# Output products of a feed-forward half: new planner ranks for the left blocks' parts and for squares and stores of a finished tile

## The chip, the cores and the metric

The kernel runs on one core of one Trainium2 chip. TensorE (PE) multiplies, VectorE (DVE) and ScalarE (ACT) work on tiles in SBUF and PSUM, GpSimd (POOL) and SyncE (SP) mostly issue DMAs. Each engine works through its own list of instructions in order. The metric is the time of one execution on the device, in microseconds; smaller is better. Three runs of the kernel before gave 2675.55, 2676.26 and 2680.1 us, a median of 2676.26 us.

## The reference

One layer of a diffusion backbone on 1024 latent tokens and 256 context tokens, width 1024. A feed-forward half, a mixer of a gated short convolution and attention, and a second feed-forward half, each behind an RMS norm with a shift, scale and gate. Cut to what matters here:

```python
def rms_norm(x, g):
    y = xf * lax.rsqrt(jnp.mean(xf * xf, axis=-1, keepdims=True) + EPS)
    return (y * g.astype(jnp.float32)).astype(x.dtype)

def swiglu(h, w_in, w_out):
    a, b = jnp.split(h @ w_in, 2, axis=-1)
    return (jax.nn.silu(a) * b) @ w_out          # D_FF = 2816 -> 1024

x = x + 0.5 * ml[2] * swiglu(modulate(rms_norm(x, norm1_g), ml[0], ml[1]), ffn1_w_in, ffn1_w_out)
... # mixer: reads rms_norm(x, norm2_g)
x = x + 0.5 * ml[8] * swiglu(modulate(rms_norm(x, norm3_g), ml[6], ml[7]), ffn2_w_in, ffn2_w_out)
return rms_norm(x, final_g)
```

The change touches the products with `w_out` of the two feed-forward halves and, in the first, what follows when a tile of the new `x` is done: its store to DRAM and its square, which the mixer's norm sums up.

## The kernel before, in words

**Numbers.** All products are in float32 with float32r operands. An operand is split into two parts: a rounded high part, made by a cast on ACT, and the rest, made by a subtraction on DVE (`split`, line 197). A product is then three matmuls: high by high, high by low, low by high. So every operand block costs one cast on ACT and one subtraction on DVE before PE can use it.

**The output product.** `row_products` computes `hidden @ w_out` (hidden dimension 2816 = 22 blocks of 128, 1024 tokens, 1024 outputs) in Winograd's form with seven half-size products instead of eight, in the order 2, 1, 4, 6, 5, 7, 3. Each product runs over 11 block rows `j`; a block row has a left block (of the weights, or of a sum of weight quarters) and a right block (of the hidden values, or of a sum of their quarters), both 128x512. PE does 12 matmuls per block row: four output tiles, three matmuls each. `operands` yields, for each pair of block rows, the parts of the left block (tiles `wl` and `wh`, alternating) and of the right block (tiles `rh` for the cast and `rl` for the subtraction; in product 3 other tiles). The left blocks of products 2, 1, 4 and 7 are loaded by SP into `raw` (7 forms a difference of two loads on DVE). Those of 5, 6 and 3 come from `ws`: a load by SP and accumulating DMAs by POOL, and for 6 and 3 a negated copy on ACT between them (`ws<-ws`). `sums` forms the sums of hidden quarters in place (`hid<-hid,hid`) and issues the `ws` steps. When a product ends, `add` on DVE (`x<-ps,gate_l,x`) adds its four PSUM tiles, scaled by the gate, to the tiles of `x` that it belongs to.

**After a product, first half only.** `after1` is called after each pair of block rows and at the end of each product. When the last product for a group of four tiles of `x` has been added, `done` stores each tile to DRAM on SP (`xd<-x`) and calls `mix.square`: a square on ACT into a tile named `sq_acc` (the first of a token block) or `sq`, and for all but the first and the last an addition to `sq_acc` on DVE. C0 and C1 are the two blocks of 512 tokens; `done` is called after product 1 for tiles 0 to 3 of C0, after product 7 for tiles 4 to 7 of C0 and of C1, and after product 3 for tiles 0 to 3 of C1. The norm of C0 (`norms2`) begins after product 7, that of C1 (`norm1`) inside the mixer's first products, after product 3. The second half calls `row_products` with `after3`, which has no squares of this kind; its last product is done in two halves.

**What sets the order.** The instructions are not issued in the order of the text. A planner replays the program on a model of the engines and places them greedily: when an engine comes free, of the instructions that are ready the one with the lowest rank goes next. The rank is a running number in the order of the text. Inside `tc.high_priority(n)` the numbers begin n below the running number (above it for a negative n), and behind the block counting goes on from where it was before it. The list of each engine is fixed then; on the chip an instruction that has to wait holds up what is behind it on the same engine. Two things bind the planner beside data. Where `strict[0]` is set (around `sums`), an instruction is pinned behind the one before it in the text on its engine. And tiles live in slots: a tile gets a slot of its tag when its first writer is placed, and the slots of one tag go out in the order in which the text names the tiles. `rh`, `rl`, `sq`, `sq_acc` and other small tiles share the tag "t" of `tpool` with 11 slots; `wl` and `wh` have 4 slots each, `raw` has 3. A slot is free again when the last reader of its tile is done.

```python
tpool = ctx.enter_context(tc.tile_pool(name="tpool", bufs=11))
def ttile(name, n=512, dt=F32):
    t = tpool.tile([P, 512], dt, tag="t", name=uniq(name))
```

Nearly all instructions go through one helper, so the profile shows them all on line 90; they are told apart by engine and tiles.

Of the kernel before, what the change touches and what calls it, by code (L numbers as in the profile page):

```python
# [35 lines left out]
C0, C1, CC = ("l", 0, 512), ("l", 512, 512), ("c", 0, CT)  # L36
# [9 lines left out]
TOKENS_AT = 5  # L46
RESIDENT, AH2, AH3 = 2, 9, 9
SLOT = 1024


@with_exitstack
def tile_dit_layer(
# [44 lines left out]
    act, dve, pool, pe, sp = (Engine(e) for e in (nc.scalar, nc.vector, nc.gpsimd, nc.tensor, nc.sync))  # L97
# [11 lines left out]
    def uniq(s):  # L109
        n_tiles[0] += 1  # L110
        return f"{s}_{n_tiles[0]}"

    def atile(name, shape=(P, SLOT), dt=F32):
        return apool.tile(list(shape), dt, tag="A", name=uniq(name))

    def ttile(name, n=512, dt=F32):
        t = tpool.tile([P, 512], dt, tag="t", name=uniq(name))
        return t[:, :n]
# [25 lines left out]
    def load(out, in_, pinned=False):  # L144
        inst = sp.dma_start(out=out, in_=in_)
        if pinned:
            tc.keep_in_program_order(inst)
# [38 lines left out]
    def col(name, k=0):  # L186
        o = voff[name] + k
        return cols[:, o : o + 1]
# [8 lines left out]
    def split(src, hi, lo, lo_eng=None, hi_eng=None):  # L197

        if hi_eng is dve:
            dve.tensor_copy(out=hi, in_=src)  # L200
        else:
            act.copy(out=hi, in_=src)
        (lo_eng or dve).tensor_sub(out=lo, in0=src, in1=hi.bitcast(F32))
# [9 lines left out]
    def load_w(src, shape, lo_eng=None, pinned=False):  # L213

        raw = wpool.tile([P, SLOT], F32, tag="raw", name=uniq("raw"), bufs=3)
        hi = wpool.tile([P, SLOT], F32R, tag="wh", name=uniq("wh"), bufs=W_BUFS)
        lo = wpool.tile([P, SLOT], F32R, tag="wl", name=uniq("wl"), bufs=W_BUFS)
        a, b = shape
# [162 lines left out]
    def norm_gain(name, m, gname):  # L381

        g = {}
        for s in "l" if m >= 5 else "lc":
            g[s] = const.tile([P, 8], F32, name=f"{name}_{s}")
            part_gain(g[s], m, gname, s, 0, 8)
        return g
# [77 lines left out]
    def run(steps, n=None):  # L465

        if n is None:
            for _ in steps:
                pass
        else:  # L470
            for _ in range(n):
                next(steps, None)
# [18 lines left out]
    class Winograd:  # L491
# [111 lines left out]
        def parts(self, k, ch):  # L603

            t = self.r[(1, 2, 0, 3)[2 * (ch == C1) + k // 4]][k % 4]
            return t[:, 0], t[:, 1]
# [10 lines left out]
        def lefts(self, pairs, side_from):  # L617

            def cols(src):
                t = wpool.tile([P, SLOT], F32, tag="raw", name=uniq("raw"), bufs=3)  # L620
                load(t[:].rearrange("p (k n) -> p k n", n=P), src.rearrange("(k p) n -> p k n", p=P))
                return t[:, :512], t[:, 512:]

            def half_cols(src, half):
                t = wpool.tile([P, SLOT], F32, tag="raw", name=uniq("raw"), bufs=3)[:, :512]
                src = src[half * 512 : (half + 1) * 512]
                load(t.rearrange("p (k n) -> p k n", n=P), src.rearrange("(k p) n -> p k n", p=P))
                return t
# [191 lines left out]
    def row_products(w, rows, add, after=lambda i, k: None, halves=False):  # L820
# [18 lines left out]
        def part_of_w(*kmlr):  # L839
            t = wpool.tile([P, 2, 512], F32, tag="raw", name=uniq("raw"), bufs=3)[:, : kmlr[1]]  # L840
            load(t, block(*kmlr))
            return t
# [4 lines left out]
        def parts(src, where):  # L847

            if where == "t":
                t = ttile("rh", dt=F32R), ttile("rl", dt=F32R)  # L850
            else:
                if where == "kept":
                    t = atile("kept", (P, 2, 512), F32R)
                else:
                    t = wpool.tile([P, 2, 512], F32R, tag=where, name=uniq(where), bufs=W_BUFS)
                t = t[:, 0], t[:, 1]
            split(src, *t)
            return t

        def blocks(k):  # L860
            return (rows.t[k, v, c] for v in range(2) for c in range(2))
# [41 lines left out]
        def operands(i, k, m):  # L903

            b11, b12, b21, b22 = blocks(k)
            if i in (1, 2, 4):
                left = part_of_w(k, m, i != 1, i == 4)
            elif i == 7:
                left, a21 = part_of_w(k, m, 0, 0), part_of_w(k, m, 0, 1)
                dve.tensor_sub(out=left, in0=left, in1=a21)  # L910
            else:
                left = (s1 if i == 5 else s2)[k]
            right = {1: b11, 2: b21, 4: b21, 5: b11, 6: b11, 7: b12, 3: b22}[i]
            for e in range(m):
                if i != 3:
                    where = ("wl", "wh")[(k + e) % 2], "t"
                else:
                    where = ("kept", "kept") if halves else ("wl", "wh")
                yield parts(left[:, e], where[0]), parts(right[:, e], where[1])
        def step(i, ps, j, l, r, ds=range(4), a=0, n=512):  # L920

            on = i in (6, 7)
            xh, xl = (t[:, a : a + n] for t in r)
            for d in ds:
                wh, wl = (t[:, d * P : (d + 1) * P] for t in l)
                matmul(ps[d], wh, xh, start=not on and j == 0, stop=False, on=on)
                matmul(ps[d], wh, xl, start=False, stop=False, on=on)
                matmul(ps[d], wl, xh, start=False, stop=j == rows.n - 1, on=on)
# [6 lines left out]
        for i in (2, 1, 4, 6, 5, 7) + (() if halves else (3,)):  # L935
            ps = chain if i in (1, 6, 7) else [ps_s() for _ in range(4)]
            for g, (k, m) in enumerate(groups):
                for e, lr in enumerate(operands(i, k, m)):
                    if e == 0:
                        fetches(i, g)  # L940
                    step(i, ps, k + e, *lr)
                strict[0] = True
                sums(i, g)
                strict[0] = False
                after(i, k)
            for o, ch in to[i]:
                for d in range(4):
                    add(o + d, ch, ps[d])
            after(i, rows.n)
# [20 lines left out]
    xs, xc = Latents("x"), Context("xc")  # L970
# [57 lines left out]
    def column_pairs(w, offsets):  # L1028
        return [tuple(w[:, o : o + P] for o in ab) for ab in offsets]
# [33 lines left out]
    xd = dram.tile([KD, P, L], F32, name="xd")  # L1063
# [6 lines left out]
    for k in range(4):  # L1070
        if k % 2:
            half1.shifted(h0[k][:, 0], k, xh[k])
        else:
            dve.tensor_scalar(
                out=h0[k][:, 0], in0=xh[k], scalar1=gain1["l"][:, k : k + 1], scalar2=modl[:, k : k + 1],
# [158 lines left out]
    for d in range(0, KD, 2):  # L1234
# [8 lines left out]
        for e in range(2):  # L1243
            te = t[:, e * CT : (e + 1) * CT]
            dve.scalar_tensor_tensor(
                out=te, in0=pt[:, e * CT : (e + 1) * CT], scalar=gate1["c"][:, d + e : d + e + 1], in1=te, op0=ALU.mult, op1=ALU.add
# [11 lines left out]
    xs = Latents("x1")  # L1258
    mix = Winograd(xs, None, modl, 3, column_pairs(wi, mix_offsets), plain=True, ahead=AH2)
# [10 lines left out]

    def after1(i, k):
        def done(ds, ch):
            for d in ds:
                sp.dma_start(out=xd[d, :, ch[1] : ch[1] + 512], in_=xs(d, ch))
                mix.square(d, ch)

        if (i, k) in residual:
            ch, d0 = residual[i, k]
            for d in range(d0, d0 + 4):
                sp.dma_start(out=xs(d, ch), in_=xd[d, :, ch[1] : ch[1] + 512])  # L1280
        if (i, k) == (5, 0):
            gain2.update(norm_gain("gain2", 3, "g2"))
            mix.gain = gain2["l"]
        if k == NH // 2:
            if i == 1:
                done(range(4), C0)
            elif i == 7:
                done(range(4, KD), C0)
                run(norms2, 1)
                done(range(4, KD), C1)  # L1290
            elif i == 3:
                done(range(4), C1)
        if i == 3 and k in (0, 4):
            run(norms2, 1)
# [23 lines left out]
    for i in range(KD):  # L1318
# [6 lines left out]
        for ch, bg, gc in mixed():  # L1325
# [4 lines left out]
            for j in (0, 2):  # L1330
# [3 lines left out]
                    out=ya, in0=u[:, a + j - 1 : b + j - 1], scalar=col(f"w{j}", i), in1=ya, op0=ALU.mult, op1=ALU.add  # L1334
# [42 lines left out]
    for kt in range(10):  # L1377
        ch = CC if kt < 2 else C0 if kt < 6 else C1
# [324 lines left out]
    xs = Latents("x2")  # L1703
# [3 lines left out]
    for ch in (C0, C1):  # L1707
        o = ch[1]
        for d in range(KD):
# [7 lines left out]
                out=xs(d, ch), in0=ps, scalar=modl[:, 40 + d : 41 + d], in1=xs(d, ch), op0=ALU.mult, op1=ALU.add  # L1717
# [12 lines left out]
        out=gf[:], in0=cols[:, voff["gf"] : voff["gf"] + 8], scalar1=math.sqrt(D), scalar2=None, op0=ALU.mult  # L1730
# [132 lines left out]
```

## Time and profile before

| what | value |
|---|---|
| median of three runs | 2676.26 us |
| the profiled execution, its own time | 2677.21 us |
| its span, first to last instruction | 2675.3 us |
| mean granted clock of TensorE | 0.995 |
| first half's output products (2, 1, 4, 6, 5, 7, 3) | about 678 to 899 us |
| second half's output products | about 2438 us to the end |

The page gives the busy time of each engine, then its share of the span. PE is a matmul, PEld the load of its weights. A row of a group or of the timeline reads `output<-inputs` by the names of tiles; `rh<-hid` is the cast of a right block, `rl<-hid,rh` its subtraction, `wl<-raw` and `wl<-raw,wl` the same for a left block, `sq<-x` a square. A timeline row has the start, the length, engine, line, operation, tiles, shapes and count, and in brackets the idle time of its engine ahead of it with what ended it. A row of waits has total, times and the longest. PEclk, in the table of stretches the number after the engines, is the granted clock as a share of full speed. The releaser "PE ps" of a cast is a matmul whose end frees the slot for which the cast waits.

### The profile page before, as it was taken

How to read it: one execution, taken by the hardware profiler on the slowest of the kernel's cores; microseconds unless marked ns; L12 is line 12 of the kernel's file. 1: busy time of each engine (PE TensorE's matmuls, PEld its weight loads, DVE VectorE, ACT ScalarE, POOL GpSimd, SP SyncE). 2: the span in 40 equal slices, each digit the busy share in tenths (PEclk: the TensorE clock that was granted, in tenths of full speed). 3: DMA queues.
4: the chain of work that ended last, by engine and by line, in shares of the span. 5: the costliest groups of instructions: out<-in, count | busy, mean ns of one | idle time of the engine just before them, and what ended most of it. 6: DMA issues, size and time to landing. Idle time of an engine off the chain costs nothing.

```text
span 2675.3 us, 36939 instructions
## 1 busy us (share of the span) xinstructions
PE 2637.8 (99%) x13373; PEld 2222.0 (83%) x13373; DVE 2007.0 (75%) x3356; ACT 1172.3 (44%) x2317; POOL 557.1 (21%) x449
## 2 busy tenths in 40 slices
PE   8999999999999999999999999999999999999998
PEld 6787799888778878888999888888888788888888
DVE  5788976788877899877588676685458876667885
ACT  6532454333453643333355576574236333334443
POOL 0134201211010044332033122141001442320200
PEclk9999999999999999999999999999999999999999
DMA  8566475345974345332522432113524543228841
GB/s 316 196 190 191 141 227 165 108 131 197 300 188 110 114 157 173 114 126 79 201 66 94 91 95 61 35 42 99 164 87 146 181 153 93 89 87 284 189 90 64
DMA packets 369744, 376.93 MB, mean 141 GB/s; under 512 B 19334, under 2 KB 258072, under 8 KB 369560
## 3 DMA queue, kind: packets, MB, share of 16 engines
q1 hardware_dynamic: 358744, 353.03, 40.7%
q0 software_dynamic: 10816, 21.53, 4.9%
q8 instruction: 105, 1.72, 0.3%
q14 instruction: 79, 0.65, 0.1%
HBM read 306.78 MB, written 67.67 MB: 140 GB/s over the span
## 4 chain that ended last, share of the span: by engine, by line
PE 92%; DVE 4%; issue 1%; DMA 1%; ACT 1%; POOL 0%; SPq 0%; DVEq 0%; POOLq 0%; ACTq 0%
PE ps L90 76%; PE po L90 8%; PE pt L90 8%; DVE r L90 1%; DVE wl L90 1%; DVE nt L90 0%; DVE macc L90 0%; DMA rawm<-in_w_mod_dram 0%; DVE uc L90 0%; POOL s L90 0%; DMA raw<-in_ffn_w_in_dram 0%; DMA ws<-in_ffn_w_out_dram 0%; DVE v L90 0%; DVE y L90 0%; DMA mcol<-mrow 0%
## 5 line engine op out<-in xcount | busy, mean ns | idle before, releaser
L90 PE MATMUL ps<-r,wl 128*128 128x512 f32 x5196 | 1206.9, 391 | 10.6 <-DVE wl L90 5.2
L90 PEld LDWEIGHTS ps<-r,wl 128*128 128x128 f32 x5196 | 973.6, 188 | 220.1 <-DVE wl L90 7.7
L90 ACT CAST wl<-s 128x512 fp32r<-128x512 f32 x254 | 156.8, 620 | 322.2 <-PE ps L90 225.1
L90 POOL TENSOR_TENSOR s<-raw 128x512 f32<-128x512 f32 x64 | 91.9, 1436 | 891.3 <-DMA raw<-in_ffn_w_in_dram 583.5
L90 ACT CAST wl<-raw 128x512 fp32r<-128x512 f32 x287 | 177.5, 620 | 219.1 <-PE ps L90 157.6
L90 DVE TENSOR_TENSOR wl<-raw,wl 128x512 fp32r<-128x512 f32 x287 | 202.4, 706 | 62.5 <-ACT wl L90 59.7
L90 DVE TENSOR_TENSOR wl<-s,wl 128x512 fp32r<-128x512 f32 x254 | 230.7, 909 | 18.3 <-ACT wl L90 16.9
L90 POOL TENSOR_TENSOR s<-raw,s 128x512 f32<-128x512 f32 x64 | 103.9, 1624 | 363.2 <-DVE wl L90 363.2
L90 DVE SCALAR_TENSOR_TENSOR macc<-rawm,silu_c,macc 128x512 f32<-128x512 f32 x178 | 149.7, 858 | 12.5 <-DMA rawm<-in_w_mod_dram 11.7
L90 PE MATMUL ps<-wh,r 128*128 128x256 f32 x768 | 141.6, 284 | 0.0
L90 DVE TENSOR_TENSOR u<-u,ps 128x512 f32<-128x512 f32 x174 | 118.3, 680 | 29.0 <-PE ps L90 28.9
L90 DVE TENSOR_TENSOR pts<-pt,pts 128x512 fp32r<-128x512 f32 x160 | 108.7, 687 | 40.8 <-ACT pts L90 39.0
L90 ACT CAST pts<-pt 128x512 fp32r<-128x512 f32 x160 | 93.3, 595 | 86.5 <-PE pt L90 82.6
L90 ACT CAST rh<-hid 128x512 fp32r<-128x512 f32 x132 | 81.3, 620 | 109.5 <-PE ps L90 94.5
L90 DVE TENSOR_REDUCE m<-ps 128x1 f32<-128x512 f32 (+1 forms) x192 | 110.3, 595 | 24.1 <-PE ps L90 20.4
L90 PE MATMUL ps<-rh,wl 128*128 128x512 f32 x360 | 123.1, 392 | 2.8 <-ACT rh L90 2.8
L90 PEld LDWEIGHTS ps<-wh,r 128*128 128x128 f32 x768 | 120.8, 192 | 0.7 <-issue 0.6
L90 ACT CAST wh<-raw 128x512 fp32r<-128x512 f32 (+1 forms) x85 | 67.9, 801 | 102.1 <-PE ps L90 71.8
L90 PE MATMUL po<-pts,vh 128*128 128x512 f32 x256 | 110.0, 435 | 0.2 <-ACT pts L90 0.2
L90 PE MATMUL ps<-wl,r 128*128 128x256 f32 x384 | 109.0, 284 | 0.0
L90 DVE TENSOR_TENSOR rl<-hid,rh 128x512 fp32r<-128x512 f32 x132 | 90.1, 686 | 22.8 <-PE ps L90 13.4
L90 PE MATMUL ps<-kl,qs 128*128 128x512 f32 x384 | 104.2, 395 | 0.0
(314 smaller groups left out, 5117.4 us busy)
## 6 DMA issues: line engine op xcount, KB each, us to landing
raw<-in_ffn_w_in_dram SPq DMA_DIRECT2D x130, 512.0 KB
raw<-in_ffn_w_out_dram SPq DMA_DIRECT2D x72, 512.0 KB
raw<-in_w_in_dram SPq DMA_DIRECT2D x61, 512.0 KB
rawm<-in_w_mod_dram SPq DMA_DIRECT2D x104, 256.0 KB
hid<-hd SPq DMA_DIRECT2D x40, 512.0 KB
rawm<-in_w_mod_dram SPq DMA_DIRECT2D x32, 512.0 KB
ws<-in_ffn_w_out_dram POOLq DMA_DIRECT2D x30, 512.0 KB, 6.5
ucd<-uc SPq DMA_DIRECT2D x25, 512.0 KB
```

The source lines that it names most:

```text
L90: inst = getattr(self.engine, name)(*args, **kw)
```

## The change

`row_products`, and so both halves: the split of a left block is placed inside `tc.high_priority(60)`, so that its cast and its subtraction are ranked 60 numbers earlier than the text would have them. The split of the right block stays. `after1`, the first half: for two of the four groups of finished tiles, tiles 0 to 3 of C0 (after product 1) and tiles 4 to 7 of C1 (after product 7), the stores, the squares and their additions are ranked 300 numbers later. The other two groups stand in a block with offset 0. Nothing is added or removed: no load, matmul or other instruction.

```diff
+AHEAD_OF = 60
+LATER = 300
@@ row_products, operands
-                yield parts(left[:, e], where[0]), parts(right[:, e], where[1])
+                with tc.high_priority(AHEAD_OF):
+                    left_parts = parts(left[:, e], where[0])
+                yield left_parts, parts(right[:, e], where[1])
@@ after1
         def done(ds, ch):
-            for d in ds:
-                sp.dma_start(out=xd[d, :, ch[1] : ch[1] + 512], in_=xs(d, ch))
-                mix.square(d, ch)
+            late = (ch == C0) == (ds[0] == 0)
+            with tc.high_priority(-LATER if late else 0):
+                for d in ds:
+                    sp.dma_start(out=xd[d, :, ch[1] : ch[1] + 512], in_=xs(d, ch))
+                    mix.square(d, ch)
```

## The prediction

> **What bounds the kernel now.** I read the page first: the share of busy time, then the chain that ended last.
>
> ```profile
> span 2675.3 us, 36939 instructions
> PE 2637.8 (99%) x13373; PEld 2222.0 (83%) x13373; DVE 2007.0 (75%) x3356; ACT 1172.3 (44%) x2317; POOL 557.1 (21%) x449
> PE 92%; DVE 4%; issue 1%; DMA 1%; ACT 1%; POOL 0%; SPq 0%; DVEq 0%; POOLq 0%; ACTq 0%
> ```
>
> TensorE bounds the kernel, and the change removes no matmul. All it can win are waits of PE in the stages that it reorders. So the second view is the table of stretches, cut by products: four of the first output half (products 2, 1, 4, 6), then two stretches of the second.
>
> ```profile
> 680.50:711.50 31.00, 29.77 (x136) 24.31 (x135) 24.62 (x43) 12.08 (x22) 1.34 (x1) 1.00 0.96 339
> 711.50:744.80 33.30, 30.03 (x133) 24.19 (x131) 30.89 (x43) 15.75 (x29) 3.67 (x3) 1.00 0.82 233
> 744.80:776.50 31.70, 31.70 (x132) 25.89 (x133) 21.00 (x30) 15.79 (x25) 5.81 (x5) 0.95 0.90 231
> 776.50:807.00 30.50, 28.73 (x126) 23.15 (x125) 27.27 (x39) 14.48 (x28) 7.03 (x6) 1.00 0.58 101
> 2470.00:2500.00 30.00, 30.00 (x134) 24.84 (x133) 29.67 (x41) 15.10 (x25) 4.22 (x4) 1.00 0.91 237
> 2500.00:2530.00 30.00, 30.00 (x134) 24.86 (x133) 22.02 (x32) 15.06 (x25) 6.43 (x6) 1.00 0.79 166
> ```
>
> Columns: length, then PE, PEld, DVE, ACT and POOL busy (with counts), granted clock, DMA share. In the second half PE is busy all 30 us in 30, with 134 matmuls, 0.224 us each: nothing to win there, only to lose. In the first half it idles, and in the third row it ran at a granted clock of 0.95. Third view, PE's waits between 680 and 870 us (total, times, longest):
>
> ```profile
> PE ps L90 <- ACT rh L90: 2.8, 1, 2.8
> PE pt L90 <- DVE rl L90: 1.8, 2, 1.4
> PE pt L90 <- ACT wl L90: 1.2, 1, 1.2
> PE pt L90 <- DVE wl L90: 0.4, 1, 0.4
> ```
>
> That is 6.2 us in all; the clock adds 0.05 x 31.7 = 1.6 us. So the reordered stages can give back some 7.8 us of 2677, 0.3%. I call under 0.2%, 5.35 us, no change: about what a measurement of this kernel can tell.
>
> **The largest wait, between products 1 and 4: the demoted squares.** Order of ACT, then of PE and DVE, around it:
>
> ```profile
> 725.67 0.62 ACT L90 CAST rh<-hid 128x512 fp32r<-128x512 f32 x1 [1.32 <-PE ps L90]
> ...
> 735.11 0.62 ACT L90 CAST wl<-raw 128x512 fp32r<-128x512 f32 x1 [4.74 <-DMA raw<-in_ffn_w_out_dram]
> ...
> 740.74 0.63 ACT L90 ACTIVATE sq_acc<-x 128x512 f32<-128x512 f32 x1 [0.84 <-DVE x L90]
> 742.05 0.62 ACT L90 CAST wl<-raw 128x512 fp32r<-128x512 f32 x1 [0.67 <-PE ps L90]
> 742.57 1.66 ACT L90 ACTIVATE sq<-x 128x512 f32<-128x512 f32 x3
> 744.14 1.12 ACT L90 CAST rh<-hid 128x512 fp32r<-128x512 f32 x2
> ```
>
> ```profile
> 744.80 1.20 PE L90 MATMUL ps<-rh,wl 128*128 128x512 f32 x4 [2.84 <-ACT rh L90]
> 745.94 0.80 PE L90 MATMUL ps<-rl,wl 128*128 128x512 f32 x1
> ...
> 746.96 0.63 PE L90 MATMUL ps<-rl,wl 128*128 128x512 f32 x1
> 747.39 0.63 PE L90 MATMUL ps<-rh,wl 128*128 128x512 f32 x1
> ```
>
> ```profile
> 742.54 0.74 DVE L90 SCALAR_TENSOR_TENSOR x<-ps,gate_l,x 128x512 f32<-128x512 f32 x1
> 743.20 0.68 DVE L90 TENSOR_TENSOR wl<-raw,wl 128x512 fp32r<-128x512 f32 x1
> 743.80 1.48 DVE L90 TENSOR_TENSOR sq_acc<-sq_acc,sq 128x512 f32<-128x512 f32 x2
> 745.20 1.28 DVE L90 TENSOR_TENSOR rl<-hid,rh 128x512 fp32r<-128x512 f32 x2
> ```
>
> It looks made for the change: three squares (1.66 us) stand right ahead of the cast for which PE waits. But look at the hole before them. The last right part of product 1 is cast at 725.67; in the 18 us after it ACT has left parts and squares alone, idles 4.74 us in one piece, and casts no right part of product 4 until 744.14, behind the fourth square. A rank cannot hold back a ready instruction from an idle engine; a slot can. Squares (`sq`) and right parts (`rh`, `rl`) are tiles of one tag, "t", with 11 slots, and the planner gives the slots of a tag in the order in which the program names the tiles, whatever their ranks. The squares are named first, so the right parts queue for slots behind them, and they can be written only once product 1's adds are done. A rank 300 lower changes neither. While the right parts are barred ACT has little else ready, so the four squares still run as soon as their `x` is there. I take 0 for the wait. Ends: +0.66, one promoted left subtraction (743.20 - 742.54) between the adds, which makes the last square that much later; and -4.4, the wait and the clock, if the squares did step aside (first rival).
>
> What the demotion does move is on DVE and SP. The three additions into `sq_acc` (two in the 743.80 row, a third behind) fall behind `rl`, which can start when its cast ends, 744.74 instead of 745.20. PE's first `rl` matmul then follows the four ahead of it at 0.224 us each, 745.70 instead of 745.94: -0.2 us. The three squares hold slots until the additions run; that leaves 7 of 11, three pairs. When those are used up DVE runs dry and does the additions, so this throttles the look-ahead for a few us and costs PE nothing. The four stores fall behind the loads in SP's queue. They are 1 MB, 4.5 us at the 233 GB/s of this stretch, moved into the next with its DMA share of 0.90; nothing reads them before the second half, and PE's wait here is for no load: 0.
>
> After product 7 the demoted squares are those of the far half of the second token block. PE's next wait after product 6 is one at 955.67 (quoted below), ACT is 44% busy overall, and the next tiles of tag "t" are wanted only after product 3, 30 us on: 0. If that cover were gone, the norm of that block would start later by four squares, 0.63 + 1.66 = 2.3 us, and with it all that waits for it in the mixer's first units.
>
> **The left parts, 60 ranks up.** Each is a cast on ACT and a subtraction on DVE, 11 to a product, 77 in each half; the load on SP and the differences that DVE forms for product 7 keep their ranks. A block row is 12 matmuls, 4 instructions of its parts and a share of the sums, so sixty ranks are three to four block rows: where a left part and a right part are ready together, the left one now goes first. Elsewhere that moves a right part by one cast, 0.5 us, and is hidden by a look-ahead of several block rows. First where that helps, the start of product 1:
>
> ```profile
> 709.83 0.62 ACT L90 CAST rh<-hid 128x512 fp32r<-128x512 f32 x1 [2.10 <-PE ps L90]
> 710.35 0.61 ACT L90 CAST wl<-raw 128x512 fp32r<-128x512 f32 x1
> ...
> 711.02 1.22 DVE L90 TENSOR_TENSOR hid<-hid,hid 128x1024 f32<-128x1024 f32 x1
> ...
> 712.81 0.68 DVE L90 TENSOR_TENSOR wl<-raw,wl 128x512 fp32r<-128x512 f32 x1
> ```
>
> PE waits 1.23 us for that `wl` cast and 0.43 us for its subtraction. The cast goes ahead of the right part: 710.35 - 709.83 = -0.52 (ends 0, if the load lands only then, and -1.23). The subtraction need not stand behind `hid` and the add, 712.81 - 711.02 = 1.8 us earlier, so the 0.43 goes whole; next late is the odd block's `wh`. Together -0.95.
>
> Then where it hurts, product 6, whose left parts hang on accumulating DMAs, so that `rl` ends just as PE wants it:
>
> ```profile
> 782.11 0.69 DVE L90 TENSOR_TENSOR rl<-hid,rh 128x512 fp32r<-128x512 f32 x1
> 782.72 0.69 DVE L90 TENSOR_TENSOR wl<-ws,wl 128x512 fp32r<-128x512 f32 x1
> ...
> 789.24 0.68 DVE L90 TENSOR_TENSOR rl<-hid,rh 128x512 fp32r<-128x512 f32 x1
> 789.84 0.68 DVE L90 TENSOR_TENSOR wl<-ws,wl 128x512 fp32r<-128x512 f32 x1
> ```
>
> At both of PE's `rl` waits a left subtraction stands right behind the late `rl`; promoted, it stands in front: 0.60 us later (789.84 - 789.24). The second inherits the first's delay of PE, so the two together cost +0.6, not 1.2. Ends 0 and +1.2. In the second half the tightest `rl` I find has 1.6 us to spare, so 0.6 there costs nothing:
>
> ```profile
> 2527.78 0.68 DVE L90 TENSOR_TENSOR rl<-hid,rh 128x512 fp32r<-128x512 f32 x1
> ...
> 2530.09 0.39 PE L90 MATMUL pt<-rl,wl 128*128 128x512 f32 x1
> ```
>
> **Sum.** -0.2 - 0.95 + 0.6 = -0.55 us. The profiled execution took 2677.21 us (its span and 1.9 around it), which gives 2676.7; it lies 0.95 above the median of the runs, 2676.26, so I say 2675.7.
>
> **Rivals.** *The squares do step aside* (chance 0.2). For it: in the second half, which has no squares there, PE never waits. Then the 2.84 wait, the 1.6 of the clock and, since the whole chain of `ws` starts earlier, product 6's 1.8 go, with -0.95 and -0.2: -7.4, 2668.9. Against it: the hole from 725.67 to 744.14.
>
> *Left casts block the right ones* (chance 0.21), slower. ACT works in order. If the planner takes an accumulating DMA to land sooner than it does, a promoted cast of the next pair stands ahead of a right cast of this one and waits for its landing.
>
> ```profile
> 778.82 1.21 POOL L90 DMA_DIRECT2D ws<-in_ffn_w_out_dram  x1 [5.47 <-issue]
> 785.10 2.16 POOL L90 DMA_DIRECT2D ws<-in_ffn_w_out_dram  x2 [5.07 <-issue]
> ```
>
> These are 6.28 us apart. It decides from the point where one whole pair is overtaken: the right part is late by up to 6.28, of which 1.4 is waited now: +4.9, and 1.6 if the clock falls again: +6.5, 2682.8; the second half, with 1.6 to spare, could add 4.7. Against it: pairs are six us apart, and sixty ranks decide only among instructions that are ready together, on an engine half idle.
>
> *The clock* (0.15, within the share of no change). Matmuls start 0.43 us apart after the 2.84 us wait (746.96, 747.39), but a wait of nearly the same length cost no slow stretch:
>
> ```profile
> 955.67 0.50 PE L90 MATMUL ps<-r,wl 128*128 128x512 f32 x1 [2.79 <-DVE wl L90]
> ```
>
> So the 1.6 us may fall away without any other change: 2674.1. The Trainium skill ("TensorE: Matmul & The Clock Gate", Part 1) says the gate halves the clock after about 3.4 us of idleness in a window that runs freely, so that its phase decides; by that rule both waits are too short to be sure of either outcome, and the time would be 2674.1 or 2675.7. The trace agrees on the half rate (0.43 against 0.224 us) and shows both outcomes.
>
> **Numbers.** Forecast and its neighbours, 2672 to 2680: 0.56 with the clock's case. Faster by over 0.2%: 0.21, nearly all the first rival. Slower: 0.23, the second rival and 0.02 for a later norm. The range reaches to both, 2668 to 2685.
>
> **What would show it.** Right: no right cast between product 1's last and the fourth square; a PE wait of 2.2 to 3.5 us on `rh` there; `sq_acc` additions behind `rl`; the waits on `wl` at product 1's start gone or halved; windows of the second half still full. Wrong: right casts running through the end of product 1 (first rival), or ACT waiting on a `ws` DMA with right casts behind it and PE idle over 3 us in product 6, in either half (second rival).

## Result and the profile after

Over 22 runs each, the changed kernel took 2681.36 us in the median (2675.58 to 2684.94), the kernel before 2677.27 us (2673.22 to 2684.45). The ratio is 1.0015 with a 95% interval of 1.0009 to 1.0022: slower by 4.1 us. That is inside the range forecast and inside the 0.2% that the prediction called no change, but its sign is wrong, 0.55 us faster having been forecast. The profiled execution took 2683.85 us.

The page of the changed kernel, span and busy times as before:

```profile
span 2682.1 us, 36941 instructions
PE 2639.0 (98%) x13373; PEld 2221.8 (83%) x13373; DVE 2003.9 (75%) x3356; ACT 1170.8 (44%) x2317; POOL 557.8 (21%) x449
```

PE is the bound as before, with the same 13373 matmuls in the same order. Now the table of stretches of the changed kernel, for products 1, 4 and 6 of the first half, then for three stretches of the second half, which begin with products 4, 6 and 5; the last of them ends in product 7 (length; PE, PEld, DVE, ACT, POOL busy; granted clock; DMA share; GB/s):

```profile
711.20:744.50 33.30, 30.05 (x132) 24.20 (x130) 30.89 (x43) 15.79 (x29) 3.67 (x3) 0.99 0.81 223
744.50:776.20 31.70, 31.58 (x132) 25.70 (x132) 19.52 (x27) 13.88 (x22) 5.80 (x5) 0.95 0.88 237
776.20:807.90 31.70, 29.05 (x124) 23.18 (x125) 29.01 (x42) 16.44 (x31) 7.04 (x6) 1.00 0.62 106
2501.30:2531.30 30.00, 30.00 (x134) 24.76 (x132) 18.59 (x28) 12.43 (x20) 5.78 (x5) 1.00 0.77 156
2531.30:2561.30 30.00, 29.52 (x129) 23.88 (x128) 26.14 (x40) 13.49 (x26) 7.03 (x6) 1.00 0.61 105
2561.30:2610.00 48.70, 48.14 (x211) 39.27 (x210) 45.54 (x68) 25.38 (x47) 3.38 (x3) 1.00 0.44 103
```

And the last two stretches in the kernel before, at the same matmuls:

```profile
2530.00:2560.00 30.00, 30.00 (x134) 24.83 (x133) 29.90 (x44) 15.28 (x28) 6.56 (x6) 1.00 0.61 106
2560.00:2608.70 48.70, 48.70 (x216) 40.36 (x215) 40.22 (x60) 22.33 (x40) 2.64 (x3) 1.00 0.37 92
```

In the first half product 1 has the same 33.3 us as before, and product 4 the same 31.7 us and the same clock of 0.95; only product 6 took 1.2 us more, 31.7 us instead of 30.5. The second half, where the kernel before was full, loses more: ten matmuls fewer fit into the last two stretches, 10 x 0.224 = 2.2 us.

**The first half.** PE's waits from 680 to 870 us in the changed kernel, and ACT's rows at the border of products 1 and 4:

```profile
PE ps L92 <- ACT rh L92: 2.8, 1, 2.8
PE pt L92 <- DVE rl L92: 1.7, 2, 1.4
PE pt L92 <- ACT wl L92: 1.2, 1, 1.2
PE pt L92 <- ACT rh L92: 1.1, 1, 1.1
PE pt L92 <- DVE wl L92: 0.4, 1, 0.4
```

```profile
740.45 0.64 ACT L92 ACTIVATE sq_acc<-x 128x512 f32<-128x512 f32 x1 [0.84 <-DVE x L92]
741.76 0.62 ACT L92 CAST wl<-raw 128x512 fp32r<-128x512 f32 x1 [0.67 <-PE ps L92]
742.28 1.66 ACT L92 ACTIVATE sq<-x 128x512 f32<-128x512 f32 x3
743.85 1.12 ACT L92 CAST rh<-hid 128x512 fp32r<-128x512 f32 x2
```

Square, left cast, three squares, right casts, each to within 0.02 us of its old place beside its neighbours: the demotion moved none of them. In the traces of the whole first half the lists of PE, ACT, POOL and SP are those of the kernel before, and on DVE three instructions move by one or two places. One row of waits is new, 1.1 us on `rh` at the start of product 6, and it makes most of the 1.2 us that product 6 took longer. The list alone cannot have made it, since a run with the same first-half list (the first experiment) does not have it.

**The second half.** There 91 places of ACT's list hold another instruction than before, 10 of SP's and 43 of DVE's. What that does to the accumulating DMAs (`ws`, issued by POOL) is seen in two places. First, SP's first load of a `ws` tile and POOL's first three accumulating DMAs, before, then after:

```profile
2455.91 1.08 SPq L90 DMA_DIRECT2D ws<-in_ffn_w_out_dram  x1
2467.09 1.24 POOL L90 DMA_DIRECT2D ws<-in_ffn_w_out_dram  x1 [45.29 <-DMA ws<-in_ffn_w_out_dram]
2475.02 1.24 POOL L90 DMA_DIRECT2D ws<-in_ffn_w_out_dram  x1 [6.69 <-issue]
2481.76 1.21 POOL L90 DMA_DIRECT2D ws<-in_ffn_w_out_dram  x1 [5.51 <-PE ps L90]
```

```profile
2459.75 0.37 SPq L92 DMA_DIRECT2D ws<-in_ffn_w_out_dram  x1
2470.02 1.24 POOL L92 DMA_DIRECT2D ws<-in_ffn_w_out_dram  x1 [46.88 <-PE ps L92]
2479.93 1.24 POOL L92 DMA_DIRECT2D ws<-in_ffn_w_out_dram  x1 [8.67 <-DMA ws<-in_ffn_w_out_dram]
2489.86 1.21 POOL L92 DMA_DIRECT2D ws<-in_ffn_w_out_dram  x1 [8.68 <-issue]
```

At this place PE itself is 1.34 us behind the kernel before. The first load is 3.84 us later, so 2.5 us beyond that. From the second accumulating DMA to the third it takes 9.93 us instead of 6.74. Second, what DMA queues moved while that second one was under way, before, then after (packets, MB, share of 16 engines' time; `q0` carries POOL's accumulating DMA of 0.52 MB, `q1` the loads of SP):

```profile
q0 software_dynamic: 272, 0.52, 59.3%
q1 hardware_dynamic: 334, 0.65, 27.1%
```

```profile
q1 hardware_dynamic: 1049, 2.03, 65.9%
q0 software_dynamic: 272, 0.52, 31.3%
```

The same 0.52 MB got half the share of the engines, beside three times as many bytes of loads: it has slipped into the burst of raw and `ws` loads that SP issues for the next block rows. The Trainium skill ("DMA: Bandwidth & Descriptors", section "Queues, rings and completion order") says that each DMA engine takes turns between the queues that have work, a packet at a time; these shares agree with it, though no run here tests it apart.

From there it goes to PE through ACT. The two negated copies (`ws<-ws`) that wait, in the kernel before, then rows of ACT and of PE in the changed kernel:

```profile
2513.83 1.06 ACT L90 ACTIVATE ws<-ws 128x1024 f32<-128x1024 f32 x1 [2.18 <-DMA ws<-in_ffn_w_out_dram]
2522.27 0.63 ACT L90 ACTIVATE ws<-ws 128x512 f32<-128x512 f32 x1 [6.36 <-DMA ws<-in_ffn_w_out_dram]
```

```profile
2520.71 1.06 ACT L92 ACTIVATE ws<-ws 128x1024 f32<-128x1024 f32 x1 [6.91 <-DMA ws<-in_ffn_w_out_dram]
...
2522.19 0.61 ACT L92 CAST rh<-hid 128x512 fp32r<-128x512 f32 x1
2528.30 0.63 ACT L92 ACTIVATE ws<-ws 128x512 f32<-128x512 f32 x1 [5.50 <-DMA ws<-in_ffn_w_out_dram]
```

```profile
2531.96 0.50 PE L92 MATMUL pt<-rl,wl 128*128 128x512 f32 x1 [0.37 <-DVE rl L92]
2601.26 0.50 PE L92 MATMUL pt<-rl,wh 128*128 128x512 f32 x1 [0.56 <-DVE rl L92]
```

The two copies waited before, too, 2.18 and 6.36 us; now they wait 6.91 and 5.50 us and run 5.5 and 4.7 us later, counted from PE's place. Right casts of product 6 stand behind them in ACT's list. The look-ahead that the second half lived on is used up and PE stops for `rl`, in product 6 and again in product 7. A stop costs more than the wait in brackets: the matmul at 2531.96 starts 0.76 us after the one before it, the next one 0.34 us, where 0.23 is usual. Counted so, the stops in product 6 cost 1.0 us and those in product 7 1.1 us.

In product 7 DVE waits 2.5 us for a `raw` load, after a stretch from 2562 to 2585 us in which it has no pause. That this goes back to the late chain is argued only: run 6 below has a late chain and no stop in product 7, and DVE waits as long there in runs 1 and 4 (2.7 and 2.6 us) without a stop.

### The profile page after: what moved, and what is told of

Read it like the earlier page. It is cut to its first block, busy times and chain, and to the rows that moved or that the text cites. A ratio compares the mean times of both kernels' runs of the same rounds, so it can differ in the third digit from the quotient of the medians.

```text
span 2682.1 us, 36941 instructions
## 1 busy us (share of the span) xinstructions
PE 2639.0 (98%) x13373; PEld 2221.8 (83%) x13373; DVE 2003.9 (75%) x3356; ACT 1170.8 (44%) x2317; POOL 557.8 (21%) x449
## 4 chain that ended last, share of the span: by engine, by line
PE 54%; issue 2%; DVE 1%; DMA 1%; ACT 0%; POOL 0%; DVEq 0%; POOLq 0%; ACTq 0%; SPq 0%
PE ps L92 45%; PE po L92 5%; PE pt L92 4%; DMA ws<-in_ffn_w_out_dram 1%; POOL ws L92 0%; DMA raw<-in_ffn_w_out_dram 0%; DVE r L92 0%; DVE wl L92 0%; DVE nt L92 0%; DVE uc L92 0%; ACT pts L92 0%; DVE pts L92 0%; ACT q L92 0%; ACT pl L92 0%; DVE m L92 0%
## 5 line engine op out<-in xcount | busy, mean ns | idle before, releaser
L92 PE MATMUL ps<-rh,wh 128*128 128x512 f32 x300 | 102.3, 389 | 0.0
```

The source lines that it names most:

```text
L92: inst = getattr(self.engine, name)(*args, **kw)
```

## The experiments

All of them beside the kernel before on the same chip. Two executions with the same list differ by a few us, so the table stands first: what the traces show, stage by stage, worked out from the start of the same matmul in each trace and in that of the kernel before (us; positive is later or longer). The columns on the DMAs are starts in the second half, less the lag that PE has at 2500 us.

```
                                  first  second  last |  first    1st     2nd     3rd
                                  half's half's  30us | ws load  accum.  accum.  accum.
before                            0.00   0.00   0.00  | 2455.9  2467.1  2475.0  2481.8
changed                          +1.14  +2.23  +3.16  | 2458.4  2468.7  2478.6  2488.5
1  squares later only            -0.97   0.00   0.00  | 2455.6  2466.6  2474.7  2481.4
2  left ranks, second half       -0.74  +0.76  +1.59  | 2458.6  2468.9  2477.6  2488.0
3  ... products 2, 1             -2.06  +3.06  +1.59  | 2458.0  2468.4  2478.4  2488.6
4  ... products 5, 6, 7, 3       -1.26   0.00  +1.59  | 2456.1  2466.6  2475.2  2482.0
5  changed, chain earlier        -1.40  +2.29  +1.59  | 2455.2  2464.8  2475.1  2483.3
6  before, chain later           -1.31  +7.94  +1.59  | 2459.7  2469.3  2478.2  2485.7
7  squares named later           -4.64   0.00  +1.62  | 2456.7  2467.1  2475.6  2482.3
8  7 + chain earlier, 1st half   -6.10   0.00  +0.01  | 2455.9  2467.3  2475.2  2482.0
9  ... all products but 2, 1     -1.13   0.00   0.00  | 2456.9  2467.2  2475.2  2481.9
10 chain earlier, 1st half       -2.73   0.00  +1.60  | 2456.5  2466.7  2475.8  2482.4
11 8 + left ranks                -6.18  +2.59  +0.01  | 2458.1  2468.4  2477.3  2487.4
12 7 + chain two pairs earlier   -5.59  +0.58  +0.01  | 2456.3  2466.6  2475.6  2482.1
```

"First half's" is from 678 to 899 us, "second half's" from 2500 to 2609 us, "last 30 us" what comes after 2645 us.

**1. The squares and stores alone.** Edit, against the changed kernel:

```diff
-                with tc.high_priority(AHEAD_OF):
+                with tc.high_priority(0):
                     left_parts = parts(left[:, e], where[0])
```

> Only the demotion of squares and stores; the left parts keep their ranks. The instruction lists differ from those of the kernel before in three places of VectorE's list in the first half (one sq_acc addition behind one hid sum, one rl subtraction and one sum two places later), and nowhere else. Theory (the loss is made in the second half, by the left ranks there): no change, within 0.04% of the kernel before, the wait between products 1 and 4 again 2.84 us on rh, the second half's windows full. Rival 1 (the demotion costs: the changed kernel's trace was 0.9 us behind in product 6 and 1.4 us behind by 1100 us): +1.4 us, +0.05%, with the same longer rl and rh waits in product 6. Rival 2 (the squares step aside after all): -4 us or more.

Measured: 2679.46 us, ratio 1.0003 (0.9994 to 1.0012). The wait between products 1 and 4 is 2.84 us on `rh`, the second half loses nothing. The demotion costs nothing that can be seen; the 1.06 us wait on `rh` in product 6 of the changed kernel's trace is not there, though the first half's list is the same. The first half came out 0.97 us shorter than in the kernel before; equal lists differ by more, since runs 2, 3, 4, 6 and 9 have the first half of the kernel before and came out 0.74 to 2.06 us shorter.

**2 to 4 and 9. Which left ranks.** Edits, without the demotion; in 3, 4 and 9 the condition names products:

```diff
-                with tc.high_priority(AHEAD_OF):
+                with tc.high_priority(AHEAD_OF if halves else 0):                       # 2
+                with tc.high_priority(AHEAD_OF if halves and i in (2, 1) else 0):       # 3
+                with tc.high_priority(AHEAD_OF if halves and i in (5, 6, 7, 3) else 0): # 4
+                with tc.high_priority(AHEAD_OF if halves and i not in (2, 1) else 0):   # 9
```

> Only the left ranks, and only in the second half. The lists of ScalarE, SyncE and of VectorE's second half are those of the changed kernel; VectorE's three moves in the first half are gone. Theory: as slow as the changed kernel, +2.2 us from the second half's products (PE waits on rl in products 6 and 7) and up to +4 in the median, so 0.08 to 0.17% slower than before. In the trace, the first accumulating DMA of the second half starts 1.5 to 3 us later than in the kernel before, counted from the end of the product ahead, and the sixth 5 to 6 us later; rl stands less than 0.5 us ahead of PE in product 6. Rival 1: only half of the loss, +2 us or less with the rest in the first half. Rival 2 (the loss is clock and landing scatter): within 0.04%.

> Left ranks raised only in products 2 and 1 of the second half. SyncE's list has the two raw loads moved ahead of the hid loads and ahead of the first ws load, as the changed kernel has it; the negated copies and the casts from ws keep their old places on ScalarE. Theory A (the loads moved ahead push the first ws load back, and with it the whole chain of accumulating DMAs, which run one after the other): most of the loss is here, +2 to +4 us (0.08 to 0.15%). Theory B (the negated copies and right parts stand behind left casts that wait for ws, in products 4 to 6): nothing here, within 0.04%.

> Left ranks raised only in products 5, 6, 7 and 3 of the second half: SyncE's list is that of the kernel before, on ScalarE the casts from ws go ahead of one right part and one of them ahead of the last negated copy. Theory A (the loads): within 0.04% of the kernel before, PE full in products 6 and 7. Theory B (casts from ws in front of the right parts): +2 to +4 us (0.08 to 0.15%), PE waiting on rl in products 6 and 7.

> The left ranks raised in products 4, 5, 6, 7 and 3 of the second half, not in 2 and 1: the complement of the run with 2 and 1 alone. On SyncE the first ws load keeps its place ahead of the third raw load. Theory A: the second accumulating DMA takes about 6.5 us, as before, no wait of PE in the second half's products, time within 0.05% of the kernel before. Theory B: the negated copies stand one left cast later on ScalarE and casts from ws in front of right parts, so the chain is late all the same and PE waits 1 to 2 us in product 6: +0.05 to +0.1%.

Measured: 1.0004 (0.9995 to 1.0013) for the second half's ranks, 1.0016 (1.0007 to 1.0026) for products 2 and 1 alone, 0.9999 (0.9990 to 1.0008) for 5, 6, 7 and 3, and 1.0003 (0.9994 to 1.0012) for all but 2 and 1. The time of the second run is below what was expected, though its interval does not exclude +0.1%; its trace shows a loss, 0.76 us, a third of what was expected, all in product 7. A stretch of the third (second accumulating DMA delayed), then of the ninth, at the same clock times, most of it product 4 (the ninth is 3.7 us further back in the program):

```profile
2505.00:2535.00 30.00, 28.30 (x124) 22.79 (x124) 16.99 (x25) 10.99 (x19) 5.79 (x5) 1.00 0.79 171
```

```profile
2505.00:2535.00 30.00, 30.00 (x134) 24.84 (x133) 23.72 (x34) 12.52 (x21) 5.79 (x5) 1.00 0.79 172
```

So the second half's loss comes from ranks in products 2 and 1, whose left blocks are plain loads that hang on no accumulating DMA. The ranks in products 3 to 7, where a promoted cast can stand in front of a right one and wait for `ws`, cost nothing. The table's right part divides the runs in the same way: wherever 2 and 1 are promoted (changed, 2, 3, 11) the first `ws` load is 2.1 to 2.7 us later and the third accumulating DMA 5.6 to 6.9 us; wherever they are not (1, 4, 7 to 10, 12) both are within 1.0 us of before. What links the two is SP's list: in these four, `raw` loads go ahead of `hid` loads, and one more of them than before stands ahead of the first `ws` load. The left casts stand further forward in ACT's list, so that `raw` slots come free earlier for the planner; that this is what moves the loads is argued from the two lists.

**5 and 6. The chain of accumulating DMAs moved by itself.** `e` is in place of the 3 in `sums`, which sets with which pair of block rows a `ws` tile is begun:

```diff
-            if i == 1 and g >= 3 or i == 4 and g < n - 3:
-                k, m = groups[g - 3 if i == 1 else n - 3 + g]
+            e = 3 - (2 if halves else 0)     # 5, in the changed kernel
+            e = 3 - (-1 if halves else 0)    # 6, in the kernel before
+            if i == 1 and g >= e or i == 4 and g < e:
+                k, m = groups[g - e if i == 1 else n - e + g]
```

> The changed kernel with one edit: in the second half the load and the first accumulating DMA of a ws tile stand two pairs of block rows earlier in the text, so that SyncE issues the first ws load two DMAs earlier. All left ranks are as in the changed kernel. Theory A (the accumulating DMAs run one after the other, and the changed order starts them late and into the raw loads): the sixth of them starts at least 3 us earlier than in the changed kernel, the second takes under 8 us instead of 9.7, PE is full in the second half's products 6 and 7, and the loss of 2.2 us there is gone: the time of the kernel before, within 0.05%. Theory B (the promoted casts stand in front of the right ones, wherever the chain begins): PE still waits on rl there, 1 us or more, and the time stays 0.08 to 0.15% above the kernel before.

> The kernel before with one edit: in the second half the loads and first accumulating DMAs of ws stand one pair of block rows later in the text; on SyncE the first ws load falls behind the third raw load, as in the changed kernel. No rank is changed. Theory A: the second accumulating DMA takes 9 to 10 us instead of 6.5, the sixth starts 4 to 6 us later, and PE waits on rl in product 6 or 7 of the second half, 0.7 to 3 us in all, though nothing was promoted. Theory B: PE stays full, 0.

Measured, 6: 2688.27 us, 1.0028 (1.0017 to 1.0040). No rank was touched, and the second half loses 7.9 us, more than expected. ACT and PE:

```profile
2522.73 1.06 ACT L90 ACTIVATE ws<-ws 128x1024 f32<-128x1024 f32 x1 [8.34 <-DMA ws<-in_ffn_w_out_dram]
2531.95 0.63 ACT L90 ACTIVATE ws<-ws 128x512 f32<-128x512 f32 x1 [7.13 <-DMA ws<-in_ffn_w_out_dram]
2535.26 0.79 PE L90 MATMUL ps<-rl,wl 128*128 128x512 f32 x1 [4.98 <-DVE rl L90]
```

The same two negated copies wait, 8.34 and 7.13 us, and PE 4.98 us near the end of product 4; the matmuls behind it are 0.43 us apart, at half the clock, which makes the rest. A late chain is enough by itself to stop PE around the border of products 4 and 6. The expected way was partly wrong: the second accumulating DMA took 7.45 us to the third, not 9 to 10, with 1.44 MB of loads beside it. With the 0.50 MB of run 9 (6.7 us), 0.65 MB before (6.74) and 2.03 MB after (9.93), its length grows with the bytes beside it (a longer one also has more time to meet them, so the bytes are not the whole proof).

Measured, 5: 2678.07 us, 0.9994 (0.9985 to 1.0003), which is below the changed kernel's own interval and was expected. But the expected reason failed: its trace still loses 2.29 us in the second half, in products 6 and 7. The chain began 2.3 us ahead of before, but the last `ws` tiles' first steps now stand in front of the negated ones. The negated copies have no wait of their own there; ACT's longest wait is at a promoted left cast, with a right cast behind it:

```profile
2519.47 0.62 ACT L92 CAST wh<-ws 128x512 fp32r<-128x512 f32 x1 [7.79 <-DMA ws<-in_ffn_w_out_dram]
```

So in this order the promoted casts do block, as theory B said. Whether an earlier chain cures the change stays open, and why the time does not show the trace's loss too.

**7, 8, 10 and 12. The squares' slots, and the chain in the first half.** Edits to the kernel before; `done` for the first four tiles is called after three pairs of block rows of product 4 instead of at the end of product 1:

```diff
-            if i == 1:
-                done(range(4), C0)
-            elif i == 7:
+            if i == 7:
...
+        if (i, k) == (4, 4):
+            done(range(4), C0)                # 7, 8, 12
...
+            e = 3 - (0 if halves else 1)      # 8, 10; 2 instead of 1 in 12
```

> The kernel before with one edit: the stores and squares that follow product 1 are called in the text after three pairs of block rows of product 4, so their tiles are named behind those pairs' right parts. No rank is changed. Theory (slots go out in the order of the text; the squares bar the right parts from their slots, whatever their rank): right casts of product 4 run before the end of product 1, the 2.84 us wait on rh goes and with it the slow stretch behind it, and part of product 6's waits since its negated copies come earlier: -3 to -7 us, 0.11 to 0.26% faster. Rival (the hole comes from elsewhere, from hid sums or loads): the wait stays at 2 to 3 us, within 0.04%.

> As the run before, and in the first half the ws loads and their first accumulating DMAs stand one pair of block rows earlier in the text. Theory: product 6's waits on rl in the first half (1.8 us) are of the same making as those of the changed kernel's second half, so they go too: 1 to 2 us below the run before, 5 to 8 us below the kernel before. Rival: the adds run one after the other all the same and begin when hid sums allow, so nothing beyond the run before.

> The kernel before with the ws loads and their first accumulating DMAs one pair of block rows earlier in the text of the first half, the squares where they were. Theory: the chain of accumulating DMAs is what product 6 of the first half waits for; its waits on rl (1.8 us) go, but the 2.84 us wait on rh between products 1 and 4 stays, since the squares still hold the slots: -1 to -2 us (0.04 to 0.08%). Rival: with the right parts of product 4 late the negated copies are late too, so the earlier loads buy nothing: within 0.03%, product 6 waits 1 us or more.

> Squares named later, and the first half's ws loads two pairs of block rows earlier instead of one. Theory: one pair was already enough to take product 6's wait away, so nothing more is won, within 0.05% of that run (about 0.2% faster than the kernel before). Rival: the loads now stand ahead of the hid loads on SyncE and delay product 1's operands: a longer wait at the start of product 1, +1 us or more against that run.

Measured: 7 is at 0.9985 (0.9976 to 0.9994), 8 at 0.9977 (0.9967 to 0.9987), 10 at 0.9993 (0.9984 to 1.0001), 12 at 0.9983 (0.9974 to 0.9991). Run 8, 2673.96 us beside 2679.35 us, is faster than both kernels. ACT across the border in 7:

```profile
732.73 0.62 ACT L90 CAST rh<-hid 128x512 fp32r<-128x512 f32 x1 [0.70 <-PE ps L90]
733.25 1.06 ACT L90 ACTIVATE ws<-ws 128x1024 f32<-128x1024 f32 x1
...
743.61 0.62 ACT L90 CAST rh<-hid 128x512 fp32r<-128x512 f32 x1 [1.28 <-PE ps L90]
...
746.86 0.62 ACT L90 ACTIVATE sq_acc<-x 128x512 f32<-128x512 f32 x1
```

The hole is filled: right casts and negated copies run through the end of product 1, and the first square comes at 746.86, behind six right casts. That is what the demotion by 300 ranks was to do and could not, since the squares' slots still went out first. Product 6's wait on `rl` did not go in 7; it is 2.3 us there. PE's waits from 680 to 870 us in 10:

```profile
PE ps L90 <- ACT rh L90: 2.8, 1, 2.8
PE pt L90 <- DVE wl L90: 1.6, 1, 1.6
PE pt L90 <- ACT wl L90: 1.2, 1, 1.2
```

With the chain alone earlier (10) product 6's waits on `rl` go and the 2.8 us stay; with both (8) only the two rows on `wl` are left. Of the 7.4 us that the prediction gave its first rival, 3.2 were there once the squares stepped aside (7, by the medians), and 5.4 with the chain edit as well (8). What 10 and 8 pay is a longer wait on `wl` at product 1's start, 1.6 instead of 0.4 us. Two pairs (12) bring nothing beyond one, and the start of product 1 waits 2.09 us in one piece, with a slow stretch behind it. Its second half loses 0.58 us, for which the runs show no cause.

**11. The left ranks on top of 8.**

```diff
-                yield parts(left[:, e], where[0]), parts(right[:, e], where[1])
+                with tc.high_priority(AHEAD_OF):
+                    left_parts = parts(left[:, e], where[0])
+                yield left_parts, parts(right[:, e], where[1])
```

> The run with squares named later and the first half's chain one pair earlier, and the left ranks of the changed kernel raised on top. Theory A: the first half is as in that run (no rh wait, no rl wait in product 6), and the second half loses what it lost in the changed kernel: 1 to 3 us on PE's rl waits, so 0.04 to 0.12% above that run and still about 0.12% faster than the kernel before. Rival (the left ranks also help or hurt in the first half once the squares are out of the way): the first half's waits at the start of product 1, 1.2 us on wl and 1.6 us on its subtraction, shrink by 0.5 us or more.

Measured: 2676.08 us, 0.9989 (0.9980 to 0.9998), beside 0.9977 for run 8: 0.12% lost again, as theory A expected. The first half takes as long as that of run 8 (-6.18 and -6.10 us), its waits at product 1's start still 1.2 and 1.6 us. In the second half the second accumulating DMA is slow again, 10.15 us to the third, and PE waits twice on `rl`, 1.4 us together:

```profile
2473.39 1.24 POOL L92 DMA_DIRECT2D ws<-in_ffn_w_out_dram  x1 [7.65 <-issue]
2483.54 1.21 POOL L92 DMA_DIRECT2D ws<-in_ffn_w_out_dram  x1 [8.91 <-PE ps L92]
```

## Why the prediction was wrong

The forecast was -0.55 us, the measured difference +4.1. Step by step:

- **PE bound, nothing to win in the second half, only to lose:** right, and the loss came from there.
- **The wait of 2.84 us, 0 taken:** right, to 0.01 us, and for the reason given. Runs 7 and 8 show the other side: once the squares are named later their slots go out later, and the wait is gone.
- **Additions into `sq_acc` behind `rl`, -0.2:** failed. Two of the three still run ahead of `rl`, and only the third fell behind a sum of `hid`. Worth 0.
- **Stores on SP, 0, and the squares after product 7, 0:** right; SP's and ACT's lists of the first half do not change.
- **Left parts at the start of product 1, -0.95:** failed. The waits are 1.23 and 0.42 us as before, because ACT's list there is the same. Presumably the left part's cast was not ready together with the right one for the planner, so that its rank decided nothing; the planner's own times are not on record.
- **Left parts in product 6, +0.6:** failed in the same way. The two subtractions kept their places; the 1.06 us wait in the trace is not the list's (run 1).
- **The second half, 0, with 1.62 us of slack:** this is the step that failed and cost the sign. The prediction said that "the load on SP" keeps its rank and priced a promotion as one subtraction of 0.6 us against the tightest `rl`. The rank was kept, the place was not: SP's list was made anew with the promoted casts, and `raw` loads went ahead (by way of their slots, as argued above). The first `ws` load went back by 2.5 us, and its chain into the next burst of loads. PE lost 2.23, 0.76, 3.06 and 2.59 us there in the four traces that have these lists (changed, 2, 3, 11), 2.2 us in the mean.
- **The second rival** named the accumulating DMAs and the second half, which is where the loss is. Its mechanism is a promoted left cast waiting for `ws` in front of right casts. Runs 4 and 9 show that such casts alone cost nothing, and in the changed kernel ACT's longest waits are at negated copies, which the change does not promote; run 5 shows a promoted cast blocking for 7.79 us, so with a late chain they may add to the loss. Of the price, 6.5 us and up to 4.7 more from the second half, the first half showed nothing that the list made, and the second half about half of its part.
- **The third rival, the clock,** was right in that both outcomes occur. The wait of 2.84 us is the same in ten traces; a slow stretch follows in six of them (kernel before, changed, 3, 4, 5, 9) and none in four (1, 2, 6, 10). It belongs to no list; what decides it stands at the end of this document.

Of the 4.1 us, the second half's 2.2 are shown by the traces to come with the ranks in products 2 and 1; about half of it, in product 7, is not traced to the chain. The rest stays open. The four kernels with these lists measured 0.15, 0.04, 0.16 and (run 11 against run 8) 0.12% slower, 0.12% or 3.1 us in the mean, with intervals of 0.07 to 0.13% to either side; the changed kernel's profiled execution lost a further 3.16 us in the last 30 us to the clock (below), which run 11, with the same ranks, did not.

## What to carry to other kernels

A rank moves more than the instruction that carries it: whatever waits for the slot which that instruction frees moves with it, here loads on another queue, and a load that is put off by 2.5 us can meet a burst that its neighbours had just missed. Before promoting something, follow its slots to the queue that refills them, and look for chains of DMAs that run one after the other: a late first link can make all the others late, though an earlier one did not cure it here (run 5). And where tiles of one tag get their slots in the order of the text, a rank cannot let a later tile pass; moving the lines can, and here that was worth 0.15%, with the chain 0.23%.

## What the runs showed of the hardware that was not expected

**The clock after light work.** In the last 30 us of the traces PE never waits, but the granted clock falls in some. Changed kernel, the stretch and the matmuls ahead of the slow ones:

```profile
2650.00:2664.00 14.00, 14.00 (x96) 14.00 (x95) 5.74 (x21) 1.69 (x3) 0.00 (x0) 0.76 0.28 114
```

```profile
2652.86 0.60 PE L92 MATMUL ps<-kept,kept 128*128 128x256 f32 x3
2653.30 3.15 PE L92 MATMUL pt<-ones,sq 128*128 128x1 f32 x24
2656.31 0.99 PE L92 MATMUL ps<-kept,kept 128*128 128x256 f32 x3
```

In 3.15 us PE runs 24 matmuls of a single column; busy by its rows, but doing little. Behind them three matmuls of 256 columns take 0.99 us; three of the same ahead of them took 0.60. In the kernel before that stretch ran at a clock of 1.00. Over the fourteen traces the last 30 us cost 0 more than before in six (before, 1, 8, 9, 11, 12), 1.6 us in seven and 3.2 us in one, whatever the lists. The traces' clock records speak for the light matmuls: in each trace the slow stretches start on one grid of 3.41 us. In the eight traces that lost time the single-column matmuls take 0.63 to 0.76 of one such window, and the slow stretch starts where that window ends; in the six others they are split between two windows and take at most 0.55 of either.

**Half the clock after short waits.** The stretches just behind the wait of 2.84 us, in the kernel before, then in run 10:

```profile
745.90:749.50 3.60, 3.60 (x10) 2.86 (x10) 3.60 (x6) 2.99 (x6) 1.21 (x1) 0.53 1.02 308
```

```profile
746.20:749.80 3.60, 3.60 (x16) 2.92 (x16) 3.60 (x7) 3.60 (x7) 1.22 (x1) 1.00 1.04 344
```

Ten matmuls at a clock of 0.53, or sixteen at 1.00. A slow stretch followed this wait in six of ten traces, a wait of 4.98 us (run 6), and one of only 2.09 us (run 12). The grid decides here, too: in the six traces PE is busy for 0.57 to 1.68 of the 3.41 us of the window just before the slow stretch; in the four others the wait is split between two windows, and PE is busy for at least 1.87 us in both. The Trainium skill ("TensorE: Matmul & The Clock Gate", Part 1) has the gate close after an idle window of about 3.4 us that runs freely. The waits of 2.84 and 2.09 us are shorter than such a window, so the rows do not agree with complete idleness over a window as the condition: in run 9 a window with 1.68 us busy, idle for half, was enough. The fixed grid, and an outcome that changes from one execution to the next with the same list, do agree with a window that runs freely.

**Accumulating DMAs in a row.** Each of 512 KB starts about 0.3 us after the one before has landed, so their lengths, 6.5 us beside 0.65 MB of loads and 9.7 us beside 2 MB, add up on the way to product 6.
